# Operand tiles 64 bytes behind multiples of 512, and another order of the seven-product blocks, in an encoder of two layers

## The chip, the core and the metric

The kernel runs on one core of a Trainium2 chip. Its engines are TensorE (PE, with PEld for its weight loads), VectorE (DVE), ScalarE (ACT), GpSimd (POOL) and SyncE (SP), which here issues the loads from memory. The metric is the time of one execution on the device in microseconds, the median of several runs. TensorE's clock has two levels, 1.2 and 2.4 GHz; the profile gives the level that was granted as a share of the higher one.

## What is computed

One sequence of 512 tokens with 1024 features goes through two layers and a final normalization. Each layer is a half-step SwiGLU feed-forward, a token mixer, and another half-step feed-forward; the mixer of the first is an S5 state space model beside gated linear attention, that of the second a multi-scale retention.

```python
def rmsnorm(x, g):
    return x * lax.rsqrt(jnp.mean(x * x, axis=-1, keepdims=True) + EPS) * g

def swiglu_ffn(h, w1, w2):                 # D_MODEL 1024, D_FF 2816
    gate, up = jnp.split(h @ w1, 2, axis=-1)
    return (jax.nn.silu(gate) * up) @ w2

# layer 0:  x += 0.5 * ffn1(norm(x)); x += s5_gla(norm(x));    x += 0.5 * ffn2(norm(x))
# layer 1:  x += 0.5 * ffn1(norm(x)); x += retention(norm(x)); x += 0.5 * ffn2(norm(x))
# out = rmsnorm(x, final_norm)
```

## The kernel before

Activations lie transposed: eight tiles `x[0]` to `x[7]` of 128 features by 512 tokens. A product in float32 precision is made of three matmuls in float32r (`mm3`, lines 191 to 195): each operand is split into a high part (a cast) and a low part (what the cast left), and high x high, high x low and low x high are added up in PSUM. So every weight tile needs a cast (`wh`) and a low part (`wl`). `weights` (line 171) makes the low part of most weights by `lows` (line 187): ScalarE writes the negated value, then a DMA from POOL's queue adds the raw weights to it in place. With `plain` VectorE subtracts instead. `split` (line 219) is a ScalarE cast and a VectorE subtraction.

The normed operands live in the pool `operands`, 28 tiles of 128 x 512 named `y`. `operand7` (line 109) prepares them for the three feed-forward steps that use `ffn7`: `x[0]` to `x[3]` give two tiles each, holding B11 and N1; each of `x[4]` to `x[7]` gives five, with B21, B22, N3, N2 and N4 for the pair `x[i-4]`, `x[i]`. Each tile has a high and a low half or is one of the two.

`ffn7` (line 270) replaces the eight 2 x 2 block products of the first matrix by seven (Strassen in Winograd's form), over halves of the features and of the tokens. In period j the weights are two raw units of 512 KB, `up` and `gate`, in a ring of four `raw` buffers that all weight loads share. From them come A1 (cast and low part of `up`, `ready_a1`), four sums of quarters (`sums13`, `sums24`), which are split in pairs of 1024 columns (`ready_32`, `ready_14`), and the last quarter `qh`, `ql` (`ready_22`, whose low part is made by `lows`). A product is 4 x 3 = 12 matmuls of 256 columns; a period has 84 of them. Several products add to one PSUM bank, and between them ScalarE copies the bank's state to SBUF (`saved`, line 334, tile `sv`), so that the next product of that bank waits for this copy. The order in a period of before is p1(j), r1(j-1), r3(j), r2(j), r4(j-1), p2(j), a22(j-1). The 22 periods come in three chunks (`CHUNKS`); after each chunk its part of the second matrix follows, with 512 columns a matmul and the hidden tiles `g` as moving operand.

The order of the instructions on each engine is made by a list scheduler that follows the order in the code, with some code (`tc.high_priority`) put a number of places ahead; every engine then works through its own list strictly in order, as does each DMA queue. A load into a `raw` buffer waits until everything that read it has ended, accumulate DMAs too.

The tiles lie in SBUF in the order in which their pools are opened. Their sizes are such that all float32r tiles, moving and stationary, start at multiples of 512 bytes.

The mixers end with projections that add to `x[n]` and prepare the operand tiles of the next step right behind (`prep`): in `s5_gla` by the calls of `project_out` at lines 1051 to 1061, in `retention` by the loop of line 1162.

Of the kernel before, what the change touches and what calls it, by code (L numbers as in the profile page):

```python
# [50 lines left out]
def encoder(tc, I, out, dbg=None):  # L51
# [5 lines left out]
    with ExitStack() as ctx:  # L57
# [10 lines left out]
        yp = ctx.enter_context(tc.tile_pool(name="operands", bufs=28))  # L68
        ytile = lambda dt=F32R: yp.tile([128, S], dt, name="y", tag="y")
        yh, yl = [None] * KT, [None] * KT  # L70

        columns = cp.tile([128, 96], F32, name="columns")
# [36 lines left out]
        def operand7(i, n):  # L109


            if i < 4:
                g = norm_gain(n, i)
                b, m = ytile(), ytile()
# [11 lines left out]
            bh, bl, nh, nl, m = (ytile() for _ in range(5))  # L126
# [143 lines left out]
        def ffn7(w1, w2, acc, nxt, gp, finish=None):  # L270
# [7 lines left out]
            raws, A1, P32, P14, A22, S14 = ({} for _ in range(6))  # L278
# [10 lines left out]
            def pair():  # L289
                return (gp.tile([128, 1024], F32R, name="ph", tag="ph", bufs=3),  # L290
                        gp.tile([128, 1024], F32R, name="pl", tag="pl", bufs=3))
# [15 lines left out]
            def sums24(j):  # L307
                up, ga = raws[j]
                s = S14[j]
                V.tensor_tensor(s[1][:, hi4], s[0][:, lo4], up[:, lo4], op=ALU.add)  # L310
                V.tensor_tensor(s[0][:, hi4], s[1][:, hi4], up[:, hi4], op=ALU.add)

            def ready_32(j):
                P32[j] = pair()
                split(S14[j][1], *P32[j])

            def ready_14(j):
                P14[j] = pair()
                split(S14[j][0], *P14[j])
# [25 lines left out]
            def r3(j, ks=range(4)):  # L345
                if ks[0] == 0:
                    st[j]["b7"] = bank()
                block(st[j]["b7"], P32[j], 0, "N3", True, ks)
# [22 lines left out]
            def r4(j):  # L371
                block(st[j]["b0"], P14[j], 1, "B22")
# [34 lines left out]
            for q, (ks0, ks1) in enumerate(CHUNKS):  # L407
                w2q = w2[0] if q == 0 else w2[1][q - 1]
                for j in range(ks0, ks1):
# [28 lines left out]
                    if j > 0:  # L438
                        r2(j)
# [967 lines left out]
```

## Time and profile before

| | |
|---|---|
| median of 3 runs | 2219.39 us (2217.96 to 2229.16) |
| the profiled execution, its own time | 2229.49 us |
| its span, first to last instruction | 2227.7 us |
| TensorE busy | 2115.4 us (95%), 12088 matmul records |
| VectorE busy | 1348.3 us (61%) |
| ScalarE busy | 1169.9 us (53%) |
| POOL busy | 363.4 us (16%) |
| mean granted clock of TensorE | 0.976 |

A busy matmul row is longer than its share of the pipeline, since matmuls overlap: the start of one to the start of the next is the time that it costs. An engine's idle time is put down to what came last before its next instruction. A float32 matmul leaves two records, a float32r matmul one.

### The profile page before, as it was taken

How to read it: one execution, taken by the hardware profiler on the slowest of the kernel's cores; microseconds unless marked ns; L12 is line 12 of the kernel's file. 1: busy time of each engine (PE TensorE's matmuls, PEld its weight loads, DVE VectorE, ACT ScalarE, POOL GpSimd, SP SyncE). 2: the span in 40 equal slices, each digit the busy share in tenths (PEclk: the TensorE clock that was granted, in tenths of full speed). 3: DMA queues.
4: the chain of work that ended last, by engine and by line, in shares of the span. 5: the costliest groups of instructions: out<-in, count | busy, mean ns of one | idle time of the engine just before them, and what ended most of it. 6: DMA issues, size and time to landing. Idle time of an engine off the chain costs nothing.

```text
span 2227.7 us, 31250 instructions
## 1 busy us (share of the span) xinstructions
PE 2115.4 (95%) x12088; PEld 1851.1 (83%) x12088; DVE 1348.3 (61%) x2101; ACT 1169.9 (53%) x1696; POOL 363.4 (16%) x396
## 2 busy tenths in 40 slices
PE   8998999998998989999998999999999998999998
PEld 6777888777878888997988899778888887898997
DVE  7697210178748667568766666545445469766564
ACT  7444444462667454546655354455455567455453
POOL 3332112201021010103111010211111112010101
PEclk9999999998999999999999999999999999999999
DMA  8878888967465554554555464667676765564551
GB/s 238 204 195 226 199 190 195 228 163 210 129 160 152 148 143 141 145 143 123 140 151 148 131 145 127 161 167 173 165 177 151 172 149 149 145 155 129 150 155 48
DMA packets 125364, 357.54 MB, mean 160 GB/s; under 512 B 20096, under 2 KB 34816, under 8 KB 125088
## 3 DMA queue, kind: packets, MB, share of 16 engines
q0 software_dynamic: 41328, 133.19, 32.3%
q1 hardware_dynamic: 83888, 222.36, 29.8%
q8 instruction: 95, 1.56, 0.3%
q14 instruction: 53, 0.43, 0.1%
HBM read 208.18 MB, written 14.14 MB: 100 GB/s over the span
## 4 chain that ended last, share of the span: by engine, by line
PE 59%; DMA 13%; issue 8%; DVE 7%; ACT 5%; POOL 1%; SPq 0%; ACTq 0%; DVEq 0%; POOLq 0%
PE mm L193 19%; PE mm L194 19%; PE mm L195 19%; DMA raw<-in_ffn_w_dram 6%; DMA ql<-raw 4%; DMA wl<-raw 2%; ACT wl L188 1%; ACT qh L324 1%; ACT ql L188 1%; DVE pl L221 1%; POOL wl L189 0%; ACT sv L336 0%; DVE y L134 0%; PE st L1146 0%; DVE wl L182 0%
## 5 line engine op out<-in xcount | busy, mean ns | idle before, releaser
L193 PE MATMUL mm<-y,wh 128*128 128x512 f32 (+1 forms) x1304 | 461.9, 355 | 7.7 <-ACT wh L1218 5.0
L195 PE MATMUL mm<-y,wl 128*128 128x512 f32 (+1 forms) x1304 | 458.3, 352 | 9.7 <-DMA wl<-raw 9.6
L194 PE MATMUL mm<-y,wh 128*128 128x512 f32 (+1 forms) x1304 | 458.3, 351 | 0.0
L180 ACT CAST wh<-raw 128x1024 fp32r<-128x1024 f32 (+1 forms) x227 | 232.2, 1027 | 414.0 <-issue 193.0
L189 POOL DMA_DIRECT2D wl<-raw x221 | 190.7, 864 | 1290.9 <-ACT wl L188 1115.1
L193 PE MATMUL mm<-y,ph 128*128 128x256 f32 x1056 | 309.8, 294 | 57.6 <-ACT sv L336 39.2
L194 PE MATMUL mm<-y,ph 128*128 128x256 f32 x1056 | 306.7, 291 | 2.5 <-DVE y L134 2.5
L195 PE MATMUL mm<-y,pl 128*128 128x256 f32 x1056 | 305.7, 290 | 1.8 <-DVE pl L221 1.8
L193 PEld LDWEIGHTS mm<-y,wh 128*128 128x128 f32 x1304 | 251.8, 193 | 44.8 <-ACT wh L1218 5.0
L195 PEld LDWEIGHTS mm<-y,wl 128*128 128x128 f32 x1304 | 251.3, 193 | 44.6 <-DMA wl<-raw 12.9
L194 PEld LDWEIGHTS mm<-y,wh 128*128 128x128 f32 x1304 | 252.3, 193 | 33.5 <-issue 1.4
L193 PEld LDWEIGHTS mm<-y,ph 128*128 128x128 f32 x1056 | 210.4, 199 | 63.6 <-ACT sv L336 44.3
L193 PE MATMUL mm<-g,wh 128*128 128x512 f32 (+1 forms) x672 | 258.5, 386 | 0.5 <-ACT g L220 0.5
L194 PE MATMUL mm<-g,wh 128*128 128x512 f32 (+1 forms) x672 | 258.0, 385 | 0.0
L195 PE MATMUL mm<-g,wl 128*128 128x512 f32 (+1 forms) x672 | 257.6, 384 | 0.0
L188 ACT ACTIVATE wl<-raw 128x1024 fp32r<-128x1024 f32 x221 | 232.8, 1053 | 37.7 <-PE mm L194 21.6
L194 PEld LDWEIGHTS mm<-y,ph 128*128 128x128 f32 x1056 | 210.6, 199 | 3.3 <-DVE y L134 2.9
L195 PEld LDWEIGHTS mm<-y,pl 128*128 128x128 f32 x1056 | 209.8, 199 | 2.4 <-DVE pl L221 2.4
L221 DVE TENSOR_TENSOR pl<-sums,ph 128x1024 fp32r<-128x1024 f32 x132 | 160.7, 1222 | 79.7 <-ACT ph L220 79.3
L220 ACT CAST ph<-sums 128x1024 fp32r<-128x1024 f32 x132 | 137.2, 1048 | 69.0 <-PE mm L194 53.3
L297 ACT CAST wh<-raw 128x1024 fp32r<-128x1024 f32 x66 | 69.3, 1050 | 149.3 <-DMA raw<-in_ffn_w_dram 99.1
L193 PEld LDWEIGHTS mm<-g,wh 128*128 128x128 f32 x672 | 126.2, 188 | 25.7 <-ACT g L220 1.6
(358 smaller groups left out, 3685.0 us busy)
## 6 DMA issues: line engine op xcount, KB each, us to landing
wl<-raw POOLq DMA_DIRECT2D x221, 512.0 KB, 5.5
raw<-in_ffn_w_dram SPq DMA_DIRECT2D x196, 512.0 KB, 3.9
raw<-in_w2b_dram SPq DMA_DIRECT2D x48, 512.0 KB, 3.3
raw<-in_ret_in_dram SPq DMA_DIRECT2D x48, 512.0 KB, 3.8
ql<-raw POOLq DMA_DIRECT2D x66, 256.0 KB, 4.7
raw<-in_w2a_dram SPq DMA_DIRECT2D x24, 384.0 KB, 3.7
raw<-in_ret_out_dram SPq DMA_DIRECT2D x16, 512.0 KB, 3.7
raw<-in_ab_in_dram SPq DMA_DIRECT2D x13, 512.0 KB, 4.4
```

The lines of the kernel that those rows point to most:

```text
L180: A.copy(h[:, c], raw[:, c])
L188: A.activation(l, raw, AF.Copy, scale=-1.0)
L189: G.dma_start(l, raw, accum_op=ALU.add)
L193: T.matmul(ps, lh, rh, start=first, stop=False, skip_group_check=go_on)
L194: T.matmul(ps, lh, rl, start=False, stop=False, skip_group_check=go_on)
L195: T.matmul(ps, ll, rh, start=False, stop=last, skip_group_check=go_on)
L220: A.copy(hi, src)
L221: V.tensor_tensor(lo, src, f32(hi), op=ALU.subtract)
L297: A.copy(h, up)
L324: A.copy(h, raws[j][1][:, hi4])
```

## The change

- The operand pool is allocated from the other end of SBUF, with a spacer of 104 values at its end. By this every `y` tile starts 64 bytes behind a multiple of 512. All weights, the split sums and the `g` tiles still start at multiples of 512.
- The four sums of `ffn7` are kept in three tiles: two in one of 1024 columns (`s13`), two of 512 (`s2`, `s4`), split apart (`ready_13`, `ready_2`, `ready_4`). The order in a period is now p1(j), r1(j-1), r3(j-1), p2(j), r2(j), r4(j-1), a22(j-1): the products r1, r3, r4 and a22 of a block stand a period behind its p1, p2 and r2.
- The low part of the last quarter (A22) is made by `split`, that is by VectorE, and no longer by `lows`.
- At the start of a step the weights of two blocks are asked for 250 places ahead (before: of one block, 150 places), and p1(1) stands before p2(0).
- At the end of a chunk r1 and r3 stand before the second matrix, r4 and a22 behind the first and second group of its matmuls.
- The hidden tiles and the block tiles are in two pools, opened with `reuse_waits="tile"`.
- The mixers hand over `x[n]` in another order: 0, 1, 4, 5, 2, 3, 6, 7.

```diff
-        yp = ctx.enter_context(tc.tile_pool(name="operands", bufs=28))
+        yp = ctx.enter_context(tc.tile_pool(name="operands", bufs=28, side="right"))
...
+        ytile()
+        yp.tile([128, 104], F32, name="space", tag="space", bufs=1)
...
-            def sums13(j):
+            def sums12(j):
                 up, ga = raws[j]
-                s = S14[j] = [gp.tile([128, 1024], F32, name="sums", tag="sums", bufs=2) for _ in range(2)]
-                V.tensor_tensor(s[0][:, lo4], ga[:, lo4], ga[:, hi4], op=ALU.add)
-                V.tensor_tensor(s[1][:, lo4], up[:, lo4], ga[:, lo4], op=ALU.add)
+                sums[j] = (gp.tile([128, 1024], F32, name="s13", tag="s13", bufs=1),
+                        gp.tile([128, 512], F32, name="s2", tag="s2", bufs=1),
+                        gp.tile([128, 512], F32, name="s4", tag="s4", bufs=1))
+                s13, s2, s4 = sums[j]
+                V.tensor_tensor(s13[:, lo4], ga[:, lo4], ga[:, hi4], op=ALU.add)
+                V.tensor_tensor(s2, s13[:, lo4], up[:, lo4], op=ALU.add)
...
+            def sums34(j):
                 up, ga = raws[j]
+                s13, s2, s4 = sums[j]
+                V.tensor_tensor(s13[:, hi4], up[:, lo4], ga[:, lo4], op=ALU.add)
+                V.tensor_tensor(s4, s2, up[:, hi4], op=ALU.add)
+
+            def ready_2(j):
+                P2[j] = two("r2", 512, 2)
+                split(sums[j][1], *P2[j])
+
+            def ready_13(j):
+                P13[j] = two("r13", 1024, 1)
+                split(sums[j][0], *P13[j])
+
+            def ready_4(j):
+                P4[j] = two("r4", 512, 2)
+                split(sums[j][2], *P4[j])
 
             def ready_22(j):
                 h = gp.tile([128, 512], F32R, name="qh", tag="qh", bufs=2)
                 l = gp.tile([128, 512], F32R, name="ql", tag="ql", bufs=2)
-                A.copy(h, raws[j][1][:, hi4])
-                lows(l, raws[j][1][:, hi4])
+                split(raws[j][1][:, hi4], h, l)
...
+            def r3(j):
+                st[j]["b7"] = bank()
+                block(st[j]["b7"], P13[j], 1, "N3", True)
+                st[j]["t"] = tmp("ta")
+                V.tensor_tensor(st[j]["t"][:, right], st[j]["b7"][:, left], st[j]["s4"], op=ALU.subtract)
...
-            with tc.high_priority(150):
+            with tc.high_priority(250):
                 load(0)
                 load(1)
                 ready_a1(0)
-            sums13(0)
-            sums24(0)
-            ready_32(0)
+                ready_a1(1)
+                sums12(0)
+                ready_2(0)
+                sums34(0)
+                ready_4(0)
...
+                    first, last = j == ks0, j == ks1 - 1
+                    if j == 0:
+
+                        three, rest = range(3), range(3, 4)
+                        p1(0)
+                        p1(1)
+                        p2(0, three)
+                        r2(0, three)
+                    elif j != 1:
+                        p1(j)
+                    ready_22(j)
                     if j + 2 < ks1:
                         load(j + 2)
+                    if not first:
+                        r1(j - 1)
+                        if j == 1:
+                            rs = rstd(acc)
+                        r3(j - 1)
+                    if not last and j > 0:
+                        ready_a1(j + 1)
+                    ready_13(j)
                     if j == 0:
+                        p2(0, rest)
+                        r2(0, rest)
+                    else:
+                        p2(j)
                         if not last:
+                            sums12(j + 1)
                         r2(j)
...
+                    if not first:
                         r4(j - 1)
                     if not last:
+                        ready_4(j + 1)
+                    if not first:
                         a22(j - 1)
...
                 r1(j)
+                r3(j)
                 for k in range(nk):
                     for n in range(2):
                         second(n, pss[n], ws[n], [ks0 + k], ks1)
-                    if k == 1:
-                        r4(j)
-                    if k == 2:
-                        a22(j)
+                    if k < 2:
+                        (r4, a22)[k](j)
...
-            project_out(0, 2)
             acc = new_acc()
             project_out(1, 0, acc)
+            project_out(0, 2)
+            project_out(1, 2, acc)
+            project_out(0, 3)
             project_out(1, 1, acc)
-            project_out(0, 3)
-            project_out(1, 2, acc)
             project_out(1, 3, acc)
...
-                for n2 in range(4):
+                for n2 in (0, 2, 1, 3):
                     h, l = weights(I["ret_out"][g, n2])
```

How the order moves is best seen on the engines beside TensorE. ScalarE, in one period of `ffn7` before, in a chunk's middle (`ph` are the split sums, `sv` the saved banks, `tb` the silu of a finished block, `g` its hidden tile):

```order
L297 CAST wh<-raw 128x1024
L188 ACTIVATE wl<-raw 128x1024
L324 CAST qh<-raw 128x512
L188 ACTIVATE ql<-raw 128x512
L336 COPY sv<-mm 128x256
L380 ACTIVATE tb<-ta 128x512
L336 COPY sv<-mm 128x256
L220 CAST g<-tc 128x512
L220 CAST ph<-sums 128x1024
L336 COPY sv<-mm 128x256
L220 CAST ph<-sums 128x1024
```

and ScalarE in such a period of the changed kernel (`r2h`, `r4h`, `r13h` are the high parts of the split sums):

```order
L346 COPY sv<-mm 128x256
L301 CAST wh<-raw 128x1024
L191 ACTIVATE wl<-raw 128x1024
L223 CAST qh<-raw 128x512
L223 CAST r2h<-s_5824 128x512
L346 COPY sv<-mm 128x256
L223 CAST r4h<-s_5825 128x512
L346 COPY sv<-mm 128x256
L389 ACTIVATE tb<-ta 128x512
L223 CAST r13h<-s_5823 128x1024
L223 CAST g<-tc 128x512
```

The activation that began the low part `ql` is gone, the three `sv` copies stand apart, and one of the two casts of 1024 columns has become two of 512.

VectorE in the same two places, before (`pl` the low parts of the split sums, `ul` and `ta` the sums of finished banks):

```order
L362 TENSOR_TENSOR ul<-mm,sv 128x256
L221 TENSOR_TENSOR pl<-sums,ph 128x1024
L378 TENSOR_TENSOR ta<-mm,sv 128x256
L304 TENSOR_TENSOR sums<-raw 128x512
L379 TENSOR_TENSOR ta<-ta,rs 128x512
L305 TENSOR_TENSOR sums<-raw 128x512
L310 TENSOR_TENSOR sums<-sums,raw 128x512
L381 TENSOR_TENSOR tc<-ul,tb 128x256
L382 TENSOR_TENSOR tc<-mm,tb 128x256
L369 TENSOR_TENSOR ta<-mm,sv 128x256
L311 TENSOR_TENSOR sums<-sums,raw 128x512
L221 TENSOR_TENSOR g<-tc,g 128x512
```

and changed:

```order
L373 TENSOR_TENSOR ul<-mm,sv 128x256
L311 TENSOR_TENSOR s_5823<-raw 128x512
L317 TENSOR_TENSOR s_5823<-raw 128x512
L312 TENSOR_TENSOR s_5824<-s_5823,raw 128x512
L387 TENSOR_TENSOR ta<-mm,sv 128x256
L318 TENSOR_TENSOR s_5825<-s_5824,raw 128x512
L224 TENSOR_TENSOR r2l<-s_5824,r2h 128x512
L388 TENSOR_TENSOR ta<-ta,rs 128x512
L224 TENSOR_TENSOR r4l<-s_5825,r4h 128x512
L224 TENSOR_TENSOR ql<-raw,qh 128x512
L390 TENSOR_TENSOR tc<-ul,tb 128x256
L391 TENSOR_TENSOR tc<-mm,tb 128x256
```

VectorE has the subtraction of `ql` added, and the low parts `r2l` and `r4l` come right behind the sums that they belong to.

POOL's queue, before, from the middle of a step:

```order
L189 DMA wl<-raw 128x1024
L189 DMA ql<-raw 128x512
L189 DMA wl<-raw 128x1024
L189 DMA ql<-raw 128x512
L189 DMA wl<-raw 128x1024
L189 DMA ql<-raw 128x512 x4
```

and changed, from the start of the last step to the end:

```order
L192 DMA wl<-raw 128x1024
L159 TENSOR_TENSOR sumsq<-sumsq,tb 128x512
L192 DMA wl<-raw 128x1024
L159 TENSOR_TENSOR sumsq<-sumsq,tb 128x512 x5
L192 DMA wl<-raw 128x1024 x20
L159 TENSOR_TENSOR sumsq<-sumsq,tb 128x512 x5
```

The DMAs that made `ql` are no longer there.

## Rows read from the trace of the kernel before

**Rows 1.** The page: busy engines, and the chain that ended last by engine.

```profile
PE 2115.4 (95%) x12088; PEld 1851.1 (83%) x12088; DVE 1348.3 (61%) x2101; ACT 1169.9 (53%) x1696; POOL 363.4 (16%) x396
...
PE 59%; DMA 13%; issue 8%; DVE 7%; ACT 5%; POOL 1%; SPq 0%; ACTq 0%; DVEq 0%; POOLq 0%
```

**Rows 2.** By stretch: length, busy PE, PEld, DVE, ACT, POOL, clock, DMA share, GB/s.

```profile
0.00:260.00 260.00, 238.87 (x1080) 193.74 (x1081) 184.57 (x347) 138.28 (x231) 81.72 (x74) 0.98 0.82 212
...
667.00:1046.00 379.00, 354.12 (x2389) 329.89 (x2388) 264.71 (x404) 205.21 (x310) 53.52 (x54) 0.97 0.54 144
...
1843.00:2216.00 373.00, 352.36 (x2422) 330.14 (x2422) 248.75 (x383) 196.60 (x295) 49.34 (x52) 0.97 0.50 133
...
808.10:811.20 3.10, 3.10 (x16) 3.10 (x16) 2.09 (x5) 1.93 (x3) 0.00 (x0) 0.50 1.06 216
```

**Rows 3.** Timeline of TensorE (start, duration), 256 columns, full clock: first and last of 33.

```profile
1159.80 0.28 PE L193 MATMUL mm<-y,wh 128*128 128x256 f32 x1
...
1163.64 0.28 PE L195 MATMUL mm<-y,wl 128*128 128x256 f32 x1
```

**Rows 4.** The same, 512 columns: first and last of 15.

```profile
599.76 0.39 PE L193 MATMUL mm<-y,wh 128*128 128x512 f32 x1
...
602.94 0.39 PE L195 MATMUL mm<-y,wl 128*128 128x512 f32 x1
```

**Rows 5.** The same, 256 columns at half clock: first and last of 15.

```profile
808.07 0.42 PE L193 MATMUL mm<-y,ph 128*128 128x256 f32 x1
...
811.05 0.42 PE L195 MATMUL mm<-y,pl 128*128 128x256 f32 x1
```

**Rows 6.** The same, float32 with 128 columns, two records a row: first and tenth row.

```profile
548.92 0.38 PE L891 MATMUL mm<-wm,xi 128*64 128x128 f32 x2
...
550.89 0.38 PE L891 MATMUL mm<-wm,xi 128*64 128x128 f32 x2
```

**Rows 7.** TensorE's waits: total us, times, longest.

```profile
PE mm L193 <- ACT sv L336: 39.2, 21, 3.5
```

**Rows 8.** One such wait: two rows of the chain, then ScalarE's and TensorE's timeline.

```profile
1165.06 6.73 DMA ql<-raw
1171.85 4.83 DMA raw<-in_ffn_w_dram
...
1176.76 1.04 ACT L297 CAST wh<-raw 128x1024 fp32r<-128x1024 f32 x1 [6.10 <-DMA raw<-in_ffn_w_dram]
...
1180.11 0.58 PE L193 MATMUL mm<-y,ph 128*128 128x256 f32 x1 [3.23 <-ACT sv L336]
```

**Rows 9.** TensorE's groups that read `y`, by form; each is one of three lines.

```profile
L193 PE MATMUL mm<-y,ph 128*128 128x256 f32 x1056 | 309.8, 294 | 57.6 <-ACT sv L336 39.2 <-ACT ph L220 16.4 <-ACT y L132 1.9
L193 PE MATMUL mm<-y,wh 128*128 128x512 f32 x776 | 309.5, 399 | 7.7 <-ACT wh L1218 5.0 <-ACT y L102 2.2 <-ACT wh L180 0.3
...
L193 PE MATMUL mm<-y,wh 128*128 128x256 f32 x528 | 152.4, 289 | 0.0
L193 PE MATMUL mm<-y,qh 128*128 128x256 f32 x264 | 74.9, 284 | 0.0
...
L193 PE MATMUL mm<-wh,y 128*128 128x512 f32 x160 | 62.5, 394 | 0.3 <-DVE tb L1074 0.3
```

**Rows 10.** DMA issues of the page: count, size, median us from issue to landing.

```profile
wl<-raw POOLq DMA_DIRECT2D x221, 512.0 KB, 5.5
...
ql<-raw POOLq DMA_DIRECT2D x66, 256.0 KB, 4.7
```

**Rows 11.** Timeline of VectorE in `ffn7`: steps of 1.14, 0.33 and 0.60 us.

```profile
1161.03 1.22 DVE L221 TENSOR_TENSOR pl<-sums,ph 128x1024 fp32r<-128x1024 f32 x1
1162.17 0.42 DVE L362 TENSOR_TENSOR ul<-mm,sv 128x256 f32<-128x256 f32 x1
1162.50 0.68 DVE L305 TENSOR_TENSOR sums<-raw 128x512 f32<-128x512 f32 x1
1163.10 0.42 DVE L378 TENSOR_TENSOR ta<-mm,sv 128x256 f32<-128x256 f32 x1
```

More of the change, by code (lines that the diff above doesn't have):

```diff
@@ L268, in ffn, with ffn7 @@
             return acc
-        def ffn7(w1, w2, acc, nxt, gp, finish=None):
+        def ffn7(w1, w2, acc, nxt, pools, finish=None):
             lo4, hi4 = slice(0, 512), slice(512, 1024)
-            raws, A1, P32, P14, A22, S14 = ({} for _ in range(6))
+            gq, gp = pools
+            raws, A1, P13, P2, P4, A22, sums = ({} for _ in range(7))
             st, gh, gl = {}, {}, {}
@@ L287, in load, with two @@
                     raws[j].append(raw)
-            def pair():
-                return (gp.tile([128, 1024], F32R, name="ph", tag="ph", bufs=3),
-                        gp.tile([128, 1024], F32R, name="pl", tag="pl", bufs=3))
+            def two(name, size, bufs):
+                return (gp.tile([128, size], F32R, name=name + "h", tag=name + "h", bufs=bufs),
+                        gp.tile([128, size], F32R, name=name + "l", tag=name + "l", bufs=bufs))
             def ready_a1(j):
@@ L365, in r1 @@
                 z = st[j]
-                block(z["b0"], P14[j], 0, "N1")
-                s4 = saved(z["b0"])
-                z["t"] = tmp("ta")
-                V.tensor_tensor(z["t"][:, right], z["b7"][:, left], s4, op=ALU.subtract)
+                block(z["b0"], P13[j], 0, "N1")
+                z["s4"] = saved(z["b0"])
             def r4(j):
-                block(st[j]["b0"], P14[j], 1, "B22")
+                block(st[j]["b0"], P4[j], 0, "B22")
             def a22(j):
@@ L413, in ffn7 @@
                         load(j + 2)
-                    if j == 0:
-                        three, rest = range(3), range(3, 4)
-                        r3(j, three)
-                        p2(j, three)
-                        r2(j, three)
-                    ready_14(j)
-                    ready_22(j)
-                    if j == ks0:
-                        if not last:
-                            ready_a1(j + 1)
-                    else:
-                        r1(j - 1)
-                        if not last:
-                            ready_a1(j + 1)
@@ L443, in ffn7 @@
+                    if not first:
                         r4(j - 1)
                     if not last:
-                        ready_32(j + 1)
-                    else:
-                        ws = [weights(w2q[n], True) for n in range(2)]
-                    if j > 0:
-                        p2(j)
-                    if j > ks0:
+                        ready_4(j + 1)
+                    if not first:
                         a22(j - 1)
@@ L1252, in encoder @@
         w2 = lambda i: (I["w2a"][i], I["w2b"][i])
-        with tc.tile_pool(name="steps12", bufs=1) as gp:
-            acc = ffn7(I["ffn2_w1"][0], w2(0), acc, 3, gp)
-            acc = ffn7(I["ffn1_w1"][1], w2(1), acc, 4, gp)
+        step_pools = lambda n: (tc.tile_pool(name=f"hidden{n}", bufs=1, reuse_waits="tile"),
+                                tc.tile_pool(name=f"blocks{n}", bufs=1, reuse_waits="tile"))
+        with ExitStack() as ctx3:
+            pools = [ctx3.enter_context(p) for p in step_pools(1)]
+            acc = ffn7(I["ffn2_w1"][0], w2(0), acc, 3, pools)
+            acc = ffn7(I["ffn1_w1"][1], w2(1), acc, 4, pools)
         show("ffn2")
@@ L1294, in finish @@
                 dma(to[:, t, c], xs[:, t, c])
-        with tc.tile_pool(name="step3", bufs=1) as gp:
-            ffn7(I["ffn2_w1"][1], w2(2), acc, None, gp, finish)
+        with ExitStack() as ctx3:
+            pools = [ctx3.enter_context(p) for p in step_pools(3)]
+            ffn7(I["ffn2_w1"][1], w2(2), acc, None, pools, finish)
 def _units(w, n_cols=128):
```

53 lines of the change are left out of this document (16 added, 37 removed).

## The prediction

> **What bounds the kernel now.** I read the page first [rows 1]: TensorE is busy for 95% of the span, VectorE for 61%, ScalarE for 53%, and the chain that ended last is TensorE for 59%, with DMA for 13%. Nothing else is near its limit as a mean, so the time is the number of matmuls by their step, plus the waits between them. Then the table by stage [rows 2]: the first stretch, 0 to 260 us, has the DMA engines 0.82 busy; the seven-product steps `ffn7` (667 to 1046 and 1843 to 2216 in the rows, between them a like one to 1418) have them near 0.5, VectorE busy for 265 of 379 us, 0.70, at most, and a granted clock of 0.97, so something stops TensorE there now and then.
>
> Next the step from the start of one matmul to the start of the next, in the timeline. In a dense run of 256 columns at the full clock, 32 steps go from 1159.80 to 1163.64 [rows 3]: 120.0 ns each. In a dense run of 512 columns, 14 steps go from 599.76 to 602.94: 227.1 ns each [rows 4]. At 2.4 GHz the columns alone take 106.7 and 213.3 ns, so a float32r matmul costs 13.3 and 13.8 ns more than its columns, the same for both widths. At the half clock, where the table shows 0.50 for 808.1 to 811.2 [rows 2], 14 steps go from 808.07 to 811.05 [rows 5]: 212.9 ns, just the 256 columns at 1.2 GHz, with nothing on top. And float32 matmuls, 18 records of 128 columns from 548.92 to 550.89 [rows 6], take 109.4 ns each; that is two cycles a column (106.7 ns) and 2.7 ns. So the extra 13 ns is there only where both streams of operands run at full rate (one value a cycle at 2.4 GHz). The loads of the weights lie beside the matmuls, and in the program before each float32r tile, moving or stationary, starts at a multiple of 512 bytes: whenever a matmul streams its operand while the next one's 512 bytes of weights are read, both walk through the same place modulo 512. The change moves just this.
>
> Last the waits of the `ffn7` stages [rows 7, 9]. The first matmuls of a product waited 39.2 us in 21 waits for ScalarE's `sv` copies, and 16.4 us for its `ph`, which is at the starts of `ffn7` after either mixer, from 667 and 1843 us on. One of the 21 is spelled out by the chain from 1165 to 1180 us [rows 8]: the accumulate DMA that makes the low part `ql` lasts 6.73 us, only then does the `raw` buffer come free, the next load takes 4.83 us, ScalarE stands idle 6.10 us before its cast `wh`, and behind it in its queue stand `wl`, `qh`, `ql` and at last `sv`, for which TensorE waits 3.23 us. From the start of that DMA to the end of the wait, when the next `ql` is on its way, are 15.05 us, against 84 matmuls x 120 ns = 10.08 us of work in a period.
>
> **The change part by part.**
>
> *Operand tiles at 64 modulo 512.* The matmuls that read a `y` tile [rows 9]: (1056 + 528 + 264) x 3 = 5544 with 256 columns, (776 + 160) x 3 = 2808 with 512. If the extra falls to the 2.7 ns of the float32 rows, it is 5544 x 10.6 + 2808 x 11.1 ns = 59 + 31 = 90 us. Those that read `g` stay, both operands at 0. No row shows a pair at another distance, so the bounds are 90 us and nothing; a loss isn't excluded by any row, and stands with the slower rival. I take the upper end, since the extra vanishes in both rows in which the streams are slower [rows 5, 6], less what the other queues won't let through: in the first stage 22 x 48 matmuls x 11.1 ns = 12 us would have to come where the DMA engines are 0.82 busy, of which I give up half, and 10 us in `ffn7`, where VectorE will fill nine tenths of a shorter period. **75 us.**
>
> The rule that speaks against this: the Trainium skill, "TensorE: Matmul & The Clock Gate", Step-by-step, has two independent SBUF read ports and says that loading the next tile's weights doesn't steal read bandwidth from the running matmul. By it the tiles' places cannot matter and this term is 0. The same page (section on 56 and 53.3 ns) gives about 2.5 ns on top of the columns at the full clock. The float32 rows agree with that [rows 6], the float32r rows have 13 and do not [rows 3, 4].
>
> *The low part of A22 by VectorE.* It removes in each of 66 periods ScalarE's activation for `ql`, POOL's issue and a DMA of 256 KB that takes 4.7 us to land [rows 10], and adds a VectorE subtraction of 512 columns, which steps on in 0.60 us [rows 11]. The `raw` buffer is then free a cast and a subtraction after `qh` starts rather than after a DMA of 4.7 to 6.7 us.
>
> *Sums over two periods.* VectorE's sums stay four of 512 columns; the splits become one of 1024 and two of 512 instead of two of 1024: by the steps in the rows [rows 11], 1.14 + 2 x 0.60 against 2 x 1.14, 0.06 us more. In a period VectorE then steps 9 x 0.60 + 1.14 + 5 x 0.33 = 8.2 us, the subtraction of `ql` among them; before it is 6 x 0.60 + 2 x 1.14 + 5 x 0.33 = 7.5 us. Its cover is TensorE's period (10.1 us now, about 9.2 after); if that were gone, 66 x 0.66 = 44 us would show. ScalarE loses a little. The order on ScalarE lets `wh` of two periods ahead be asked for after `r2`, and its weights are read nearly two periods later. The loop of an `up` buffer becomes accumulate DMA (5.5 us [rows 10]), load (4.83), `wh` and `wl` (twice 1.04 [rows 8]): 12.4 us over two periods, where 18 are to be had. So I take back four fifths of the 39.2 us: **31 us** (bounds 0 and 39).
>
> *The mixers' ends and the starts of `ffn7`.* The waits of 16.4 us [rows 9] stand at the first product with N3, which needs the last operand tiles; behind the first 12 matmuls the new order puts 12 more (`p1(1)`) and three quarters of `p2`, 3 to 4 us by the step of 120 ns, in part on tiles that come earlier, and the mixers hand over the heavy tiles of `x[4]`, `x[5]` earlier. The second block's weights are an extra load, cast and accumulate DMA ahead of the start, in ScalarE's and POOL's queues; they are asked for 250 places ahead, still in the mixer. I take **8 us** (bounds 0 and 16). The per-tile waits of the new pools remove no work and are counted here.
>
> *The clock.* After such waits TensorE runs at half clock: from 808.1 to 811.2 us 16 matmuls did in 3.1 us what takes 1.9 at 120 ns. A granted 0.97 over the 379 + 372 + 373 = 1124 us of `ffn7` is at most 34 us, part of it in waits where it costs nothing. With most waits gone I take **10 us** back (bounds 0 and 25).
>
> The sum is 75 + 31 + 8 + 10 = 124 us. The profiled execution took 2229.5 us (span 2227.7) and lies 10 us above the median of the runs, 2219.4. From its own time the sum leads to 2105; against the median I forecast **2097 us**, a little above 2219.4 - 124, as a part of the waits may be missing in the faster runs.
>
> **The rivals.**
>
> *The place of the tiles does nothing.* Then the 13 ns belong to float32r itself, and the rows at half clock show only that a fixed cost is hidden there [rows 5]. For it: no float32r row has another distance, and the float32 records, whose stationary slices of 256 bytes begin at 0 and at 256 modulo 512, step alike [rows 6]. Against it: a cost that belongs to the format should not vanish with the clock. What is left is 31 + 8 + 10 = 49 us: 2170. I give it 0.28. The Trainium skill's rule of the two read ports, named above, is this rival.
>
> *Nothing moves at all.* Raw loads stay late for another reason (the `wl` accumulate alone holds the buffers), and the place does nothing: 2219, within 0.5%, the least that a measurement of this kernel can tell. 0.06.
>
> *VectorE sets the period.* Each split is now a pair of ScalarE cast and VectorE subtraction in strict turn, with single buffers for `s13` and `r13`. VectorE works 7.5 us of a period of 10.1 and waits 2.5. If it keeps these waits, a period takes 8.2 + 2.5 = 10.7 us, 66 x 0.6 = 40 us more: 2260, slower. It decides from 10.1 - 8.2 = 1.9 us of waits per period on. Against it: its waits for TensorE's blocks shrink by themselves when VectorE is the later one, and `r13` is made right behind `r3` and read five blocks, 7 us, later. A worse distance of the streams would end on the same side. 0.09.
>
> **How the numbers follow.** The forecast has 0.57 (2097), the first rival 0.28 (2170), the second 0.06, the third 0.09. Low end: all the bounds together give 90 + 39 + 16 + 25 = 170, 2049, which I do not believe at once; 2055. High end: the first rival with 30 us instead of 49, 2190. That leaves out the last two and the tails of the others, some 0.2. Faster by over 0.5% (below 2208) are the first two cases with 0.84, the same 0.07, slower 0.09.
>
> **What would show it.** Right: steps of about 109 and 216 ns where `y` is read at the full clock, and still 227 where `g` is read; ScalarE's `sv` releasing TensorE for below 10 us in all; no `ql` DMA in the list of issues; starts of `ffn7` after the mixers with 4 to 5 us of waits each; a granted clock of 0.98 to 0.99 in the `ffn7` stages. Wrong: steps of 120 and 227 as before (then the first rival), steps of 109 with new waits of TensorE for VectorE's `r13l`, `r2l` or `r4l` (then the gain is given back to VectorE), or a DMA share above 0.9 with waits for `wl` in the first stage.

## The result, and the profile after

The changed kernel took 2167.9 us, median of 4 runs (2165.7 to 2170.0), beside 2218.9 for the kernel before: ratio 0.976, 95% interval 0.973 to 0.979, so 51 us faster. The forecast was 122 us faster. The time lies inside the range and 2 us from the first rival, "the place of the tiles does nothing" (2170).

The profiled execution took 2168.2 us (span 2166.4). Its page answers to [rows 1], busy engines and the chain by engine:

```profile
PE 2091.4 (97%) x12088; PEld 1819.0 (84%) x12088; DVE 1384.0 (64%) x2233; ACT 1144.9 (53%) x1696; POOL 308.7 (14%) x330
...
PE 55%; DVE 11%; DMA 6%; issue 4%; ACT 3%; SPq 1%; POOL 1%; DVEq 0%; POOLq 0%; ACTq 0%
```

TensorE leaves the same 12,088 matmul records in 24 us less busy time, POOL issues 66 instructions fewer (the `ql` DMAs), and DMA falls from 13% to 6% of the chain. The list of DMA issues has no `ql` any more. The steps come first, in TensorE's timeline (start, duration), against [rows 3] and [rows 4]: first and last of 33 matmuls with 256 columns, then of 15 with 512.

```profile
1168.38 0.28 PE L196 MATMUL mm<-n,qh 128*128 128x256 f32 x1
...
1172.15 0.28 PE L198 MATMUL mm<-n,r13l 128*128 128x256 f32 x1
...
296.13 0.39 PE L198 MATMUL mm<-y,wl 128*128 128x512 f32 x1
...
299.33 0.39 PE L197 MATMUL mm<-y,wh 128*128 128x512 f32 x1
```

32 steps in 3.77 us are 117.8 ns (120.0 before), 14 steps in 3.20 us are 228.6 ns (227.1 before). So the place of the tiles does something, but 2 ns and not 11, and for 512 columns in the wrong direction. Where an operand tile is the stationary side (`mm<-wh,y`, 512 columns), 14 steps from 1582.75 to 1586.02 us took 233.6 ns each, 6.5 more than with tiles at 0 (227.1 on average, in the run with that place below).

Now the three `ffn7` stretches, by the table of windows (length, busy PE, PEld, DVE, ACT, POOL, clock, DMA share, GB/s), which answer to [rows 2]; the third is cut as there, 1.3 us behind its start and 1 us before its last matmul with hidden tiles ends.

```profile
666.80:1019.00 352.20, 343.84 (x2398) 319.98 (x2397) 279.01 (x456) 199.05 (x314) 31.52 (x31) 1.00 0.47 136
1019.00:1367.70 348.70, 345.50 (x2386) 321.96 (x2386) 252.61 (x408) 184.80 (x286) 34.10 (x32) 0.99 0.47 134
1794.50:2154.60 360.10, 347.13 (x2421) 323.08 (x2421) 260.80 (x427) 188.15 (x295) 31.73 (x31) 0.98 0.42 120
```

The middle one of before, which [rows 2] leaves out, reads:

```profile
1046.00:1419.60 373.60, 356.34 (x2385) 331.66 (x2385) 243.33 (x372) 194.55 (x290) 49.59 (x52) 0.97 0.52 138
```

TensorE's idle time (length less busy PE) was 24.9 + 17.3 + 20.6 = 63 us before and is 8.4 + 3.2 + 13.0 = 25 us now: 38 us less. Its busy time falls by 26 us; 12 of them are the shorter 256-column steps (5,544 x 2.2 ns), the other 14 go with the granted clock (0.97 before, 0.98 to 1.00 now), as fewer matmuls run at half of it: the trace of before has 236 steps of 205 to 230 ns with 256 columns (213 at half clock [rows 5]), this one 73. VectorE, by contrast, has not run short: 279 us of 352 at most. The retention, between the second and the third, got slower: it took 422.2 us before and takes 425.5 now (its longer 512-column steps alone add some 4 us).

Last TensorE's waits, against [rows 7] (total us, times, longest):

```profile
PE mm L198 <- DMA wl<-raw: 13.3, 8, 3.8
...
PE mm L197 <- DMA wl<-raw: 6.6, 4, 4.7
PE mm L196 <- DVE ta L359: 5.8, 7, 1.3
PE mm L196 <- ACT wh L1229: 5.0, 1, 5.0
PE mm L196 <- ACT g L223: 4.3, 2, 2.7
...
PE mm L197 <- DVE b2l L134: 3.1, 3, 1.6
...
PE mm L196 <- ACT r13h L223: 0.9, 1, 0.9
```

No `sv` stands there, and of the split sums' high parts, which were named `ph`, only `r13h` with 0.9 us; before it was 39.2 and 16.4 us. What is left is `wl`, 19.9 us in all beside 16.2 before (10.0 of it ahead of the first `ffn7` from 367 us on, about as before, but also 4.8 in the first `ffn7`, where before had none), and short waits for VectorE, in `ffn7` 1.6 us at most (`b2l`). The question for the runs is which edit took the 55 us of waits away, and whether the tiles' place had any part in the time.

### The profile page after: what moved, and what is told of

The parts are those of the page before. It is cut to its first block, busy times and chain, and to the rows that moved or that the text cites. A ratio compares the mean times of both kernels' runs of the same rounds, so it can differ in the third digit from the quotient of the medians.

```text
span 2166.4 us, 31101 instructions
## 1 busy us (share of the span) xinstructions
PE 2091.4 (97%) x12088; PEld 1819.0 (84%) x12088; DVE 1384.0 (64%) x2233; ACT 1144.9 (53%) x1696; POOL 308.7 (14%) x330
## 4 chain that ended last, share of the span: by engine, by line
PE 55%; DVE 11%; DMA 6%; issue 4%; ACT 3%; SPq 1%; POOL 1%; DVEq 0%; POOLq 0%; ACTq 0%
PE mm L196 18%; PE mm L198 18%; PE mm L197 18%; DMA raw<-in_ffn_w_dram 2%; DMA wl<-raw 1%; DVE s L318 1%; DMA raw<-in_w2b_dram 1%; DVE wl L185 1%; DVE s L312 1%; DVE s L317 1%; DVE s L311 1%; ACT r13h L223 1%; SPq L761 1%; DVE r13l L224 0%; DVE st L956 0%
## 5 line engine op out<-in xcount | busy, mean ns | idle before, releaser
L196 PE MATMUL mm<-y,wh 128*128 128x512 f32 x776 | 309.7, 399 | 8.0 <-ACT wh L1229 5.0
L198 PE MATMUL mm<-y,wl 128*128 128x512 f32 x776 | 306.6, 395 | 8.6 <-DMA wl<-raw 8.6
L197 PE MATMUL mm<-y,wh 128*128 128x512 f32 x776 | 307.8, 397 | 0.1
L196 PEld LDWEIGHTS mm<-y,wh 128*128 128x128 f32 x776 | 147.2, 190 | 45.4 <-ACT wh L1229 5.0
L198 PEld LDWEIGHTS mm<-y,wl 128*128 128x128 f32 x776 | 147.1, 190 | 44.4 <-DMA wl<-raw 11.1
L197 PEld LDWEIGHTS mm<-y,wh 128*128 128x128 f32 x776 | 147.3, 190 | 34.4 <-DVE y L106 2.5
L196 PEld LDWEIGHTS mm<-g,wh 128*128 128x128 f32 x672 | 126.5, 188 | 29.2 <-ACT g L223 5.2
L198 PEld LDWEIGHTS mm<-g,wl 128*128 128x128 f32 x672 | 126.7, 188 | 25.7
L197 PEld LDWEIGHTS mm<-g,wh 128*128 128x128 f32 x672 | 126.6, 188 | 25.3 <-DVE g L224 1.1
L398 DVE SCALAR_TENSOR_TENSOR ta<-mm,rs 128x512 f32<-128x512 f32 (+1 forms) x74 | 49.8, 674 | 98.9 <-PE mm L198 98.9
L159 POOL TENSOR_TENSOR sumsq<-sumsq,tb 128x512 f32<-128x512 f32 x47 | 72.1, 1535 | 205.8 <-ACT tb L158 204.7
L346 ACT COPY sv<-mm 128x256 f32<-128x256 f32 x198 | 72.0, 364 | 43.6 <-PE mm L198 43.0
L185 DVE TENSOR_TENSOR wl<-raw,wh 128x1024 fp32r<-128x1024 f32 (+1 forms) x72 | 81.1, 1129 | 14.6 <-ACT wh L183 14.6
```

The lines of the kernel that those rows point to most:

```text
L159: G.tensor_tensor(acc, acc, sq, op=ALU.add)
L185: V.tensor_tensor(l[:, c], raw[:, c], f32(h[:, c]), op=ALU.subtract)
L196: T.matmul(ps, lh, rh, start=first, stop=False, skip_group_check=go_on)
L197: T.matmul(ps, lh, rl, start=False, stop=False, skip_group_check=go_on)
L198: T.matmul(ps, ll, rh, start=False, stop=last, skip_group_check=go_on)
L346: A.copy(z, ps[:, left])
```

## The experiments

Thirteen kernels, each timed beside the kernel before on the same chip, except the first, which was run once. In these runs the kernel before had medians of 2222.1 to 2224.1 us beside 2218.9 in the first result, so a ratio says more than a time.

### The place of the tiles

**The step by itself.** A kernel that computes nothing of the reference: blocks of 24 float32r matmuls, the moving operand `m` bytes and the weights `s` bytes behind a multiple of 512, at the full clock, nothing else running.

```diff
+for cols in (512, 256):
+    for m in PLACES:
+        run(cols, m, 0)
+    for m, s in PAIRS:
+        run(cols, m, s)
```

> Leaves out the whole encoder: 24 float32r matmuls each at many distances between the place of the moving operand and that of the weights, modulo 512 bytes, for 512 and for 256 columns. Theory A (the distance sets the step, each width in its own way): the step at distance 0 is 227 and 120 ns, at 64 bytes 230 and 118 as in the changed kernel, with the weights at 64 and the operand at 0 it is 235, and some other distance is better for both. Theory B (the place does nothing; the steps of the changed kernel moved for its other order): 227 and 120 ns at every distance.

TensorE's timeline of this kernel (start, duration, the name says columns, `m` and `s`). A step is the distance from a row's start to the next row's, over 24.

```profile
49.08 5.67 PE L73 MATMUL w512m64s0x<-mv,st 128*128 128x512 f32 x24
54.58 5.70 PE L73 MATMUL w512m80s0x<-mv,st 128*128 128x512 f32 x24
...
93.66 5.61 PE L73 MATMUL w512m256s0x<-mv,st 128*128 128x512 f32 x24
99.11 5.77 PE L73 MATMUL w512m288s0x<-mv,st 128*128 128x512 f32 x24
...
127.05 5.76 PE L73 MATMUL w512m448s0x<-mv,st 128*128 128x512 f32 x24
132.65 5.76 PE L73 MATMUL w512m480s0x<-mv,st 128*128 128x512 f32 x24
...
154.68 5.76 PE L73 MATMUL w512m0s64x<-mv,st 128*128 128x512 f32 x24
160.27 5.74 PE L73 MATMUL w512m0s128x<-mv,st 128*128 128x512 f32 x24
...
193.33 3.03 PE L73 MATMUL w256m0s0x<-mv,st 128*128 128x256 f32 x24
196.20 3.11 PE L73 MATMUL w256m4s0x<-mv,st 128*128 128x256 f32 x24
...
207.59 2.99 PE L73 MATMUL w256m64s0x<-mv,st 128*128 128x256 f32 x24
210.41 3.04 PE L73 MATMUL w256m80s0x<-mv,st 128*128 128x256 f32 x24
...
247.19 2.89 PE L73 MATMUL w256m448s0x<-mv,st 128*128 128x256 f32 x24
249.91 3.00 PE L73 MATMUL w256m480s0x<-mv,st 128*128 128x256 f32 x24
```

512 columns: 229.2 ns at 64, 227.1 at 256, 233.3 at 448, and 232.9 with the weights at 64; the other places lie between 226.7 and 236.7, and the least stand at equal places modulo 256. So the kernel before already had the best place for 512 columns, and the 13 ns on top of the columns are there at all of them. 256 columns: 119.6 ns at 0, 117.5 at 64, 113.3 at 448 (113.8 at 192, 113.3 at 112). Here a place can save up to half of the 13 ns, and 64 is a poor choice. Theory A holds.

**The place alone, both ways.** The change with its tiles back at 0 (a larger spacer), and the kernel before with its tiles at 64 (the first edit of the change alone, with its spacer of 104):

```diff
-yp.tile([128, 104], F32, name="space", tag="space", bufs=1)
+yp.tile([128, 120], F32, name="space", tag="space", bufs=1)
```

> The changed kernel with its operand tiles back at multiples of 512, all else and every engine's order as in it. Theory A: 256 columns step 120 ns again and 512 columns 227, so the three seven-product steps lose 5544 x 2 ns = 11 us and the rest wins about 8 us: 2168 + 3 = 2171 us. Theory B: steps and time as in the changed kernel, 2168 us. The forecast of the prediction would have wanted 2168 + 75.

> The kernel before with the operand tiles alone put 64 bytes behind multiples of 512. Theory A: steps of 118 ns and 230 ns (235 where the weights are the operand tile); 2219 - 3 = 2216 us. Theory B: steps of 120 and 227 ns, 2219 us. In both, the waits for the sv copies stay at about 39 us.

Measured: 2168.9 us, ratio 0.974 (0.9717 to 0.9762) with the tiles at 0, beside 0.976 for the change; and ratio 1.0009 (0.9993 to 1.0025) for the kernel before with tiles at 64. The steps moved just as in the change, the waits did not: the kernel before with tiles at 64 still waits 39.7 us for `sv`. Averaged over all steps at the full clock, 256 columns take 119.9 ns with the tiles at 0 and 117.6 at 64, 512 columns 227.2 and 229.3, and those with an operand tile as weights 227.1 and 233.3. By these steps the balance is 5,544 x 2.3 = 13 us won, 2,328 x 2.1 = 5 us and 480 x 6.2 = 3 us lost, a gain of some 5 us. The time doesn't show it: the change is as fast with its tiles at 0, and the interval of the other kernel leaves a gain of 0.07% or 1.6 us at most. So theory A holds for the steps and theory B for the time; what takes the 5 us back is not shown.

**A better place.** The two places that were best for 256 columns, by spacers of 32 and of 288 bytes:

```diff
-yp.tile([128, 104], F32, name="space", tag="space", bufs=1)
+yp.tile([128, 8], F32, name="space", tag="space", bufs=1)
```

> The changed kernel with a spacer of 32 bytes in place of 416, so that the operand tiles lie 448 bytes behind a multiple of 512 and not 64; nothing else differs. Theory A (the step hangs on the distance between the moving operand and the weights, as in the run that measured it by itself): 256-column steps 113.3 ns and not 117.5, 512-column steps that move an operand tile 233.3 ns and not 229.2, those with an operand tile as weights 229.2 and not 232.9. With 5,544 steps of the first kind, 2,328 of the second and 480 of the third that is -23 + 10 - 2 us: 2168 falls to about 2153 (2148 to 2158). Theory B (what a step gains the waits take back, as the runs with tiles at 0 and at 64 gave one time): steps as in theory A, time 2164 to 2171. Theory C (the distances in the run by itself don't carry over): steps 117.5 and 229 as in the change, time 2164 to 2171.

> The changed kernel with a spacer of 288 bytes, operand tiles 192 bytes behind a multiple of 512; nothing else differs. Theory A: 256-column steps 113.8 ns, 512-column steps moving an operand tile 232.9 ns: -21 + 9 us against the change, about 2156 (2150 to 2161). Theory B and theory C as for the tiles at 448: 2164 to 2171.

Measured: 0.9777 (0.975 to 0.9805) and 0.976 (0.9735 to 0.9785), no gain. Theory A was half right. The 512-column steps rose as expected (14 steps from 292.96 to 296.22 us at 448: 232.9 ns). The 256-column steps did not follow: at 448 only 1,101 of the trace's 5,643 took 113 or 114 ns, at 192 it was 1,681, and most of the others stayed at 117 to 119. By the averages (116.9 and 116.4 ns, beside 117.6 in the change) they win 4 and 7 us, the steps with an operand tile as weights 2, and the other 512-column steps lose 9, so nothing was to be had.

The fast steps are not strewn. A row of 256-column matmuls without a break keeps one pace: of the 42 rows of 12 or more at 448, 13 ran at 113 to 114 ns and 29 at 117 to 119, nearly from end to end; at 192 it was 18 and 27. The longest fast row, at 192: its first and last matmul, then the table of windows.

```profile
700.99 0.28 PE L196 MATMUL mm<-n23h,r2h 128*128 128x256 f32 x1
...
735.45 0.28 PE L198 MATMUL mm<-n23h,r13l 128*128 128x256 f32 x1
```

```profile
700.90:735.60 34.70, 34.70 (x309) 34.70 (x308) 33.51 (x61) 24.51 (x41) 1.72 (x2) 1.00 0.61 178
```

These 304 steps took 113.4 ns each, with VectorE busy for 33.5 of 34.7 us, ScalarE for 24.5 and the DMA engines for 0.61 of it. So the other engines' work at the same time doesn't by itself hold the step at 117. What sets a row's pace when it begins stayed open.

### What took the waits away

**The low part of A22.** First the change with this edit undone, then the kernel before with this edit alone:

```diff
-split(raws[j][1][:, hi4], h, l)
+A.copy(h, raws[j][1][:, hi4])
+lows(l, raws[j][1][:, hi4])
```

> The changed kernel with the low part of A22 made by the accumulate DMA again. Theory C (this DMA held the raw buffers, and that is what made the waits for sv): most of the 39 us of waits come back, with the half clock behind them some 45 us: 2200 to 2215 us. Theory D (the new order of the products and the weights asked for earlier took the waits away, whoever makes the low part): 2168 to 2180 us, with VectorE less busy.

> The kernel before with one edit: the low part of A22 by VectorE's subtraction and not by ScalarE's activation and an accumulate DMA. Theory Q (the ql DMA that holds a raw buffer is what makes ScalarE and its sv late): most of the 39 us of waits for sv go, and 5 to 10 us of half clock with them: 2175 to 2195. Theory O (the order of the products and sums must change too, since wh and ph stand ahead of sv in ScalarE's queue all the same): a gain like that in the changed kernel, 8 to 14 us: 2207 to 2214 against 2222.

Measured: the change without it 2179.9 us, ratio 0.9795 (0.9769 to 0.9821): 8 us of the gain go by the ratios, 12 by the times. Theory C falls, theory D holds, at the upper end of its range. The kernel before with it alone 2182.1 us, ratio 0.9801 (0.9774 to 0.9829): 41 us of the gain come with two lines. Theory Q holds, theory O falls. Taken alone it is worth far more than undone, so the two ways, this edit and the rest of the change, mostly remove the same waits. In the first, 9.4 us of waits for `sv` are back; in the second 1.6 of the 39.2 are left, and another wait leads the list. TensorE's waits of the change with the DMA, then of the kernel before with the subtraction:

```profile
PE mm L196 <- ACT sv L347: 9.4, 7, 2.9
```

```profile
PE st L163 <- POOL sumsq L156: 29.2, 2, 14.7
PE mm L195 <- DMA wl<-raw: 9.5, 6, 3.6
...
PE mm L193 <- ACT sv L335: 1.6, 5, 0.5
```

That it goes by the `raw` buffers shows on ScalarE: its waits for loaded weights at the cast `wh` of `ffn7`, in the kernel before and then in the one with the subtraction.

```profile
ACT wh L297 <- DMA raw<-in_ffn_w_dram: 99.1, 30, 6.3
```

```profile
ACT wh L297 <- DMA raw<-in_ffn_w_dram: 43.4, 27, 3.3
```

They fall by 56 us. The edit also takes an activation from ScalarE's list and a DMA from POOL's queue; what each of the three is worth was not run apart.

The middle `ffn7` stretch of the second kernel, which has no mixer ahead of it (windows, columns as above):

```profile
1032.00:1382.00 350.00, 349.22 (x2385) 325.31 (x2386) 253.69 (x388) 182.60 (x267) 32.56 (x32) 1.00 0.49 133
```

With 0.8 us idle and the full clock it takes 350.0 us beside 348.7 in the change and 373.6 before. In this stretch the new order of sums and blocks has nothing left to gain, nor have the new pools and the order at the chunks' ends, which were not run apart. The 1.3 us are less than the steps of 120 against 117.8 ns are worth (1,848 x 2.2 ns = 4 us).

**The order at the mixers' ends.** The change with the old order at both ends:

```diff
-for n2 in (0, 2, 1, 3):
+for n2 in range(4):
...
+project_out(0, 2)
 acc = new_acc()
 project_out(1, 0, acc)
-project_out(0, 2)
-project_out(1, 2, acc)
-project_out(0, 3)
 project_out(1, 1, acc)
+project_out(0, 3)
+project_out(1, 2, acc)
 project_out(1, 3, acc)
```

> The changed kernel with the old order at both mixers' ends: project_out as before, and n2 in 0, 1, 2, 3. Theory E (the new order at the ends is what lets the next feed-forward half start without its wait): the start of the first and third feed-forward halves waits 4 to 8 us each again, 2176 to 2184. Theory S (the two blocks of A11 first, and the higher priority, cover the start whatever the mixer's end): 2165 to 2172.

Measured: 2164.7 us, ratio 0.9735 (0.971 to 0.9761). Theory E falls: the old order is no slower. From the first matmul to the end of the last one with hidden tiles, the third `ffn7` was 7.7 us shorter in this trace (354.7 beside 362.4 us), the first 3.6 us longer, so the old order at the retention's end alone was tried too (the first pair of lines of the diff):

> The changed kernel with the old order at the end of the retention alone (n2 in 0, 1, 2, 3); the GLA mixer keeps its new order. The traces of the change and of the run with both old orders say: the first feed-forward half 352 us with the new order and 356 with the old, the third 364 with the new and 356 with the old. Theory R (these differences are the orders' own): 2157 to 2163, ratio 0.971 to 0.974. Theory N (they are the spread of one execution): 2164 to 2171, ratio 0.974 to 0.978.

Measured: 2160.9 us (2159.3 to 2171.2, 6 runs), ratio 0.9717 (0.9686 to 0.9748), the fastest of all. Its third `ffn7` took 355.3 us. In the four other traces that differ from the change only in the tiles' place or the second block, and so keep the new order there, it took 358.8 to 361.9. That speaks for theory R, by which this edit of the change costs time; the interval of the ratio overlaps that of the change, so in the time theory N isn't excluded.

**The start of `ffn7`.** Both kernels ask for the loads of two blocks at priority there, and for the split of the first; what the change adds under it is the second split, the sums and the splits of two of them. The change with the old priority, and the change without the second block at the head:

```diff
-with tc.high_priority(250):
+with tc.high_priority(150):
     load(0)
     load(1)
     ready_a1(0)
-    ready_a1(1)
-    sums12(0)
...
+ready_a1(1)
+sums12(0)
```

> The changed kernel with the priority of the loads and of the first split set back to 150, and the second split and the sums behind it without priority as before; the two blocks of A11 stay first. Theory S: the splits come late for the first blocks of each feed-forward half behind a mixer, 4 to 8 us each, 2176 to 2184. Theory E (the order at the mixers' ends alone covers the start): 2165 to 2172.

```diff
 p1(0)
-p1(1)
 p2(0, three)
...
-elif j != 1:
+else:
     p1(j)
```

> The changed kernel without the second block of A11 at the head: period 1's first block stands again at the head of its own period; priority and the early second split stay. Theory P (the earlier priority alone covers the starts): 2164 to 2171. Theory F (the 12 matmuls more ahead of the second product cover the split of its sums): the start of the first and third feed-forward halves waits 1.5 to 3 us more each, 2171 to 2176.

Measured: 2182.3 us, ratio 0.9819 (0.9799 to 0.984) with the old priority, 14 us more than the change, so theory S holds; and 2173.0 us, ratio 0.976 (0.9729 to 0.9791) without the second block, the ratio of the change, though an effect of the few us of theory F isn't excluded. So of the three edits for the start only the priority shows in the time. The trace with the old priority has the wait of the kernel before with the subtraction, in small:

```profile
PE mm L198 <- DMA wl<-raw: 20.5, 11, 5.4
PE st L166 <- POOL sumsq L159: 7.9, 3, 6.4
```

**The matmul that waits.** `st` is the matmul of `rstd`, which sums the squares of the rows. Two kernels on top of the one with the subtraction: `rstd` behind the second period's `r1`, as the change writes it, and this with the preamble at priority 250.

```diff
 p2(j, rest)
-rs = rstd(acc)
...
 r1(j - 1)
+if j == 1:
+    rs = rstd(acc)
...
-with tc.high_priority(150):
+with tc.high_priority(250):
     load(0)
     load(1)
     ready_a1(0)
-sums13(0)
-sums24(0)
-ready_32(0)
+    sums13(0)
+    sums24(0)
+    ready_32(0)
```

> The kernel before with two edits: the low part of A22 by VectorE, and the matmul of the squares' sums (rstd) moved from the first period's end behind the second period's r1, as it stands in the changed kernel. In the run with the first edit alone TensorE waited 14.6 and 14.7 us at this matmul for POOL's sumsq, with the products behind it ready. Theory R (this matmul only stood in the way): 96 matmuls or some 11.5 us now run ahead of it, the waits fall from 29 to 3 to 8 us, 2182 to about 2160 (2156 to 2165), as fast as the change or a little faster. Theory M (the work behind it would have waited as well, for ph, or for wl): 2170 to 2182.

> The same two edits, and the preamble of the feed-forward half (loads, first split, sums, split of N3 and N2) at priority 250 in place of 150 and none. Theory R: little is left for it, 2154 to 2165. Theory M: the splits' lateness is what holds the start, and with them earlier it goes: 2155 to 2165 here, 8 us or more below the run without the priority. Theory T (earlier splits take ScalarE and POOL from the mixer's end): some us slower than the run without, 2162 to 2175.

Measured: 2186.5 us, ratio 0.983 (0.9805 to 0.9854) for the first: theory R falls, the later line gains nothing, and the time lies above the range of theory M too. With the priority 2170.0 us, ratio 0.9758 (0.9731 to 0.9785): as fast as the whole change. That is 16 us below the run without it, which is the way of theory M and not of theory T, but the time lies above the ranges of R and M, in that of T. Whether the priority needs the later line was not run. Why the first failed is in TensorE's waits and its timeline of the first kernel:

```profile
PE st L163 <- POOL sumsq L156: 34.0, 2, 17.6
...
661.75 0.28 PE L195 MATMUL mm<-y,wl 128*128 128x256 f32 x1
678.38 1.22 PE L163 MATMUL st<-sumsq,ones 128*128 128x512 f32 x1 [16.35 <-POOL sumsq L156]
```

Though it is written later, the scheduler that orders the engines' queues still puts `st` behind the first 12 matmuls of 256 columns (the first block), where it waits with ready products behind it. By the traces there are 48 ahead of it in the kernel before, 12 in both kernels here without the priority, 36 in the change with the old priority, 60 here with priority 250, and 74 and 64 (first and third `ffn7`) in the change. The priority moves the splits of the first products ahead, so more matmuls are placed before `st`. With 60 ahead the wait is gone (TensorE's waits from 661 to 720 us):

```profile
PE mm L193 <- ACT ph L220: 3.6, 2, 2.9
...
PE st L163 <- POOL sumsq L156: 0.4, 1, 0.4
```

## Why the prediction was wrong

**The step that failed** is "Operand tiles at 64 modulo 512", with its 75 us. The runs showed steps that are 2 ns shorter with 256 columns and 2 to 6 ns longer with 512, some 5 us net, and in the time nothing (1.6 us at most in the kernel before). It rested on the sentence "the extra vanishes in both rows in which the streams are slower" [rows 5, 6], which the first rival explained as well, by a fixed cost that is hidden at half clock. The upper end of the bounds was taken on that one inference, though no row had a second place. It also took it that both operands at 0 were the worst case; for 512 columns they are the best.

**The first rival held in the time, not in the letter.** Its 2170 us met 2167.9. The place isn't without effect, though: steps of 117.8 and 228.6 ns in place of 120.0 and 227.1, and 233.6 where `y` is stationary. The Trainium skill, "TensorE: Matmul & The Clock Gate", Step-by-step, has two independent read ports, so that the load of the next weights takes no read bandwidth from the running matmul. For the time of this kernel that was the better guide. That equal places step differently from unequal ones, by up to 10 ns in the run by itself (226.7 to 236.7), does not follow from it.

**The rest of the sum** was 31 + 8 + 10 = 49 us; measured are 51, of which at most 5 are the place's.

- *The `sv` waits*, 31 forecast: all 39.2 us are gone. The chain of [rows 8] was right: the `ql` DMA held the buffer, the late `wh` held ScalarE, and `sv` stood behind. The kernel before with the subtraction alone bears it out: 1.6 us of `sv` waits are left, and ScalarE waits 56 us less for loaded weights. The share credited to the new order of sums is not needed for it: either way is nearly enough.
- *The starts*, 8 forecast: TensorE's waits in the first 30 us of the two `ffn7` behind a mixer fell from 19 to 10 us, so the total was near, but the reasons were not. Neither the order at the ends nor the second block's 12 matmuls show in the time; the priority gives 14 us. The second block's weights were no extra load either, since before loads them there too. And the wait for `ph` hid another behind it: without it, `st` waits for POOL's `sumsq`, up to 17.6 us. The prediction doesn't have this wait.
- *The clock*, 10 forecast: some 14, out of the busy times above.
- *VectorE sets the period*, 0.09: it did not. VectorE is busy for 279 of 352 us, and TensorE's longest wait for it in `ffn7` is 1.6 us (`b2l`).

Of the signs that were to tell: steps of 109 and 216 ns did not come; 227 ns where `g` is read, `sv` below 10 us, no `ql` DMA, short starts (3.5 and 6.2 us of waits) and a clock of 0.98 to 1.00 did.

## What to carry to other kernels

A price for an operation's form (the 13 ns) is no price for its operands' place: before a term of the sum rests on a mechanism that no row varies, measure the step at a dozen places in a kernel of its own; that run took 291 us and would have settled 75 of 124 us. Then measure once more in the kernel itself: at 192 and 448 the step of the run by itself came in a third and a fifth of the cases.

An accumulate DMA that reads a staging buffer is part of that buffer's time to come free; where another engine has 2 us of room in a period, a subtraction there (0.60 us) can be worth a whole reordering: two lines alone gave 41 us, the whole change 51.

In a queue in strict order, look at where a small matmul that needs the slowest chain (here the row sums) is placed, not at the line where it is written; and ask what it will wait for when the wait ahead of it is gone.

## What the runs showed of the hardware

**POOL's add waits for VectorE.** The last add of `sumsq` before an `ffn7`, with a median of 1.4 us over all such adds of this trace, took 8.15 us at both starts behind a mixer in the run with `rstd` moved. POOL's timeline, two rows, then VectorE's, three of the ten from 669.71 to 677.21 us, one behind the other without a gap:

```profile
661.31 1.37 POOL L156 TENSOR_TENSOR sumsq<-sumsq,tb 128x512 f32<-128x512 f32 x1 [1.16 <-ACT tb L155]
...
670.18 8.15 POOL L156 TENSOR_TENSOR sumsq<-sumsq,tb 128x512 f32<-128x512 f32 x1 [4.21 <-ACT tb L155]
```

```profile
670.31 0.68 DVE L311 TENSOR_TENSOR sums<-sums,raw 128x512 f32<-128x512 f32 x1
...
671.85 2.35 DVE L221 TENSOR_TENSOR pl<-sums,ph 128x1024 fp32r<-128x1024 f32 x2
...
676.53 0.68 DVE L311 TENSOR_TENSOR sums<-sums,raw 128x512 f32<-128x512 f32 x1
```

POOL's add ends at 678.33, 1.1 us after VectorE's last one of the row; spans on POOL are rough, but TensorE's `st` starts at 678.38, right behind it. The Trainium skill, "SBUF — State Buffer", Who interferes with whom, says that a VectorE instruction with two SBUF inputs contends with a GpSimd instruction that reads SBUF. The rows agree: all ten have two inputs in SBUF, and the add got through only when VectorE paused. It need not wait so long: in the kernel before an add that began at 1036.74 us took 4.17 us and ended in a gapless row, and there VectorE's instruction at 1039.68 took 1.52 us in place of 0.47. So the sums of the next stage, late and in one row, also held up the row sums of this one; with the priority they ran earlier, and the last add took 1.34 us at both starts, though one before it 5.61.

**The step hangs on the operands' distance modulo 256 bytes.** In the run by itself, 512 columns: 226.7 to 227.5 ns at equal places modulo 256, 229.2 to 229.6 at 64, 320 and 576, 232.9 and 233.3 at 192 and 448, up to 236.7 at a distance of 4 bytes. 256 columns: 119.6 to 120.0 ns at equal places, 113.3 to 113.8 at 112, 192 and 448. The best place for 512 columns is a poor one for 256. In the full kernel the 512-column steps followed, while with 256 columns at 192 and 448 whole rows ran at 113 and others at 117 to 119.
